# Opening stage of a fused backbone layer: where x is loaded, when the modulation weights are asked for, and where the first modulation chain stands

## The chip, the core and the metric

One NeuronCore of a Trainium2 chip runs the kernel. Its engines are TensorE (PE; its weight loads are PEld in the profile), VectorE (DVE), ScalarE (ACT), GpSimd (POOL) and SyncE (SP); SP, POOL and ACT also hand transfers to the core's 16 DMA engines. Each engine works through its own list of instructions in order and waits on semaphores. The metric is the device time of one launch in microseconds, lower is better.

## What is computed

One layer of a diffusion backbone on 256 latent and 256 context tokens of width 2048. The part that matters here is its start:

```python
mod = jax.nn.silu(c) @ w_mod[l] + b_mod[l]
shift, scale, gate = jnp.split(mod[:, None, :], 3, axis=-1)
mod_c = jax.nn.silu(c_ctx) @ w_mod[l] + b_mod[l]
...
h = _layer_norm(x) * (1.0 + scale) + shift
h_c = _layer_norm(ctx) * (1.0 + scale_c) + shift_c
aq, ak, av, az, bq, bk, bv, bz, bg, mga, mgb = _split_cols(h @ w_in[l])
```

Behind it come neighbourhood attention, a gated linear attention in two directions, branch gates, a merge, the output projection and a layer norm. The change touches none of that.

## The kernel before

Tokens and channels are cut in 128s; a channel tile is a k-tile (kt 0 to 15, `KT`). Every projection splits its operands into a rounded part and the rest (hi and lo) and makes three matmuls: hi by hi, hi by the weights' lo, lo by hi. `mm` (line 137) issues a matmul, `split` (L140) makes hi on ACT and lo on DVE, `load` (L146) asks SP for a weight tile (`raw`, four buffers) and splits it.

The opening runs so:

- SP asks for the four 128-row tiles of x and context (`row`, 1 MB each), then for the modulation weights of k-tile 0 in two halves (`wm0_0`, `wm0_1`, 1 MB each; `load_mod`, L186). `xt`, `row` and `wm` tiles share one pool of eight 8 KB buffers (`k8`), so later `wm` halves and some `xt` tiles wait until a `row` tile has been read.
- PE transposes x (L225) into PSUM, ACT copies it out to `xt` (L226); DVE takes the statistics of the rows (L229, L230). Reciprocal deviation and mean (`rsn`) are spread over columns, transposed on PE (`st`, L247) and copied to `stat`: the first half by DVE (L251), the second by ACT (L249).
- `normalise(kt)` (L253) makes two 512-wide passes on DVE over a part of `xt` (L255, L256).
- `modulate(kt)` (L264) makes the modulation vectors of a k-tile: 16 matmuls `gp` against the two `wm` halves (L138 by way of `mm`; the trace shows each as two), a DVE copy `gs` (L273), two transposes on PE (L275), three small DVE steps `md` (L278, L281, L282), two ACT passes `h` (L285) and a `split` into `hhi` and `hlo`.
- The key projection (L300 to L313): per k-tile seven outputs (`kp`, `K0` = 7) of three matmuls each, with weights `ak` (448 KB per k-tile, tiles `r_ak`, `h_ak`, `l_ak`). In front of k-tile kt's matmuls stands the preparation of kt+1, and the `wm` halves of kt+2 are asked for by POOL, once the `gp` matmuls that read the old contents of a buffer are done.

The order on each engine is not written by hand. A scheduler of the tile framework places the instructions from the order of the code, priorities and `tc.issue_after`, which keeps an instruction behind another one. In the text below gp0, kp0, ak1 and so on carry the number of their k-tile (kp: of the output).

```python
    for kt in range(KT):
        if kt + 1 < KT:
            pend.append(load(wak[kt + 1], P * K0, f"ak_{kt + 1}", begun))
            normalise(kt + 1)
            ...
            modulate(kt + 1)
        wh, wl = pend[kt]
```

Of the kernel before, what the change touches and what calls it, by code (L numbers as in the profile page):

```python
# [16 lines left out]
P = 128  # L17
# [69 lines left out]
def tile_backbone_layer(  # L87
# [84 lines left out]
    hlo = hpool.tile([P, 2, KT, T], F32R, tag="hlo", name="hlo")  # L172
    xh, xl = hhi[:, 0], hlo[:, 0]
# [9 lines left out]
    rows = [k8([P, D], f"row{i}") for i in range(4)]  # L183
# [6 lines left out]
    for i in range(4):  # L190
        nc.sync.dma_start(rows[i][:], xin[i])
# [25 lines left out]

    mvs = tiny([P, 4, 2], "mvs", 1)
    for i in range(4):
        cols = slice(P * i, P * i + P)  # L220
        for c in range(4):
            tp = acc(f"xt{i}_{c}")
            for k in range(4):
                kt = 4 * c + k
                nc.tensor.transpose(tp[:, P * k : P * k + P], rows[i][:, P * kt : P * kt + P], ident[:])  # L225
            evac = nc.scalar.copy(xts[c][:, :, cols], tp[:].rearrange("p (k t) -> p k t", k=4))  # L226
        st = tiny([P, 4, 6], "st")
        for c in range(4):
            nc.vector.bn_stats(st[:, c, :], rows[i][:, 512 * c : 512 * c + 512])  # L229
# [32 lines left out]
    turned = []  # L262

    def modulate(kt):  # L264
        gp = bank(f"gp{kt}")
        for q in range(2):
            wm = wms[kt, q]
            for i in range(8):
                g = 32 * (i % 4)
                with tc.issue_after(turned[-1]) if turned else nullcontext():  # L270
                    mm(gp[g : g + 32, :T], scp[:, 8 * q + i, :], wm[:, i, :], q == 0 and i < 4, q == 1 and i >= 4)
        gs = k2([P, T], f"gs{kt}")
        nc.vector.tensor_copy(gs[:], gp[:, :T])  # L273
# [599 lines left out]
```

## Time and profile before

| | |
|---|---|
| median of 3 runs | 1288.79 us (1288.2 to 1289.65) |
| profiled execution, span | 1287.8 us |
| median less that span | 1.0 us |
| PE busy | 1251.3 us (97%) |
| DVE busy | 744.9 us (58%) |
| ACT busy | 521.6 us (40%) |
| POOL busy | 87.3 us (7%) |
| read from HBM | 222.49 MB, 174 GB/s over the span |

How to read it: the span runs from the first to the last instruction of one profiled execution, and the durations below come from that one. Matmuls are pipelined, so a busy PE can still hold short gaps, and the duration of one matmul is longer than the distance to the next. The first of the page's 40 slices is the only one in which PE is less than nine tenths busy (6 tenths).

### The profile page before, as it was taken

The page shows a single profiled execution, that of the slowest core. Times are in us where ns is not written, and L with a number is a line of the kernel's source. Part 1 is how long each engine was busy: PE and PEld are TensorE (multiplying, and loading weights), DVE is VectorE, ACT ScalarE, POOL GpSimd, SP SyncE. Part 2 cuts the span into 40 slices and gives each one's busy share as a digit, 9 for nine tenths or more (in the row PEclk, how much of TensorE's full clock was granted, in tenths as well). Part 3 has the DMA queues.
Part 4 walks back from the last instruction along what each step waited for, and adds up shares of the span by engine and source line. Part 5 has one row for each costly group of instructions (what it writes and reads, how often), then busy time and mean ns, then how long its engine had stood idle before and what let it go on. Part 6 is the DMA issues. An engine that isn't in the chain of part 4 may idle for free.

```text
span 1287.8 us, 20740 instructions
## 1 busy us (share of the span) xinstructions
PE 1251.3 (97%) x8548; PEld 1124.1 (87%) x8548; DVE 744.9 (58%) x1111; ACT 521.6 (40%) x752; POOL 87.3 (7%) x120
## 2 busy tenths in 40 slices
PE   6999999999999999999999999999999999999994
PEld 4767999976678898888888999999999999999784
DVE  6733322676659456465484668865455454555576
ACT  5333322444454333332442644443444434445341
POOL 1111000111110010010020000000000000000123
PEclk8999999999999999999999999999999999999997
DMA  9997333555435325334244378875666655667652
GB/s 380 400 397 286 90 96 105 165 131 134 129 98 164 98 86 177 97 102 145 82 132 133 119 223 265 282 239 181 182 182 185 187 182 181 182 184 255 236 180 76
DMA packets 61440, 230.15 MB, mean 179 GB/s; under 512 B 7376, under 2 KB 7904, under 8 KB 56224
## 3 DMA queue, kind: packets, MB, share of 16 engines
q1 hardware_dynamic: 53424, 189.83, 47.0%
q0 software_dynamic: 7488, 38.68, 8.1%
q8 instruction: 67, 1.10, 0.4%
q10 hardware_dynamic: 432, 0.30, 0.1%
q14 instruction: 29, 0.24, 0.1%
HBM read 222.49 MB, written 2.10 MB: 174 GB/s over the span
## 4 chain that ended last, share of the span: by engine, by line
PE 88%; DVE 5%; DMA 4%; issue 2%; ACT 1%; POOL 0%; DVEq 0%; SPq 0%; ACTq 0%; POOLq 0%
PE bv L138 14%; PE mga L138 7%; PE mgb L138 7%; PE va L138 7%; PE pb L138 7%; PE kp L138 7%; PE bk L138 6%; PE bz L138 6%; PE wo L138 4%; PE qp L138 4%; PE pa L138 4%; PE az L138 3%; PE gp L138 2%; PE o L138 2%; PE s L138 2%
## 5 line engine op out<-in xcount | busy, mean ns | idle before, releaser
L138 PE MATMUL bv<-l_bv,hhi 128*128 128x512 f32 x256 | 100.0, 391 | 1.0 <-DVE l_bv L144 1.0
L138 PE MATMUL bv<-h_bv,hhi 128*128 128x512 f32 x256 | 99.7, 389 | 0.0
L138 PE MATMUL bv<-h_bv,hlo 128*128 128x512 f32 x256 | 99.6, 389 | 0.0
L138 PE MATMUL bz<-hhi,l_bz 128*128 128x256 f32 x256 | 72.6, 283 | 0.7 <-DVE l_bz L144 0.7
L138 PE MATMUL mga<-hhi,h_mga 128*128 128x256 f32 x256 | 72.4, 283 | 0.0
L138 PE MATMUL mga<-hhi,l_mga 128*128 128x256 f32 x256 | 72.4, 283 | 0.0
L138 PE MATMUL mga<-hlo,h_mga 128*128 128x256 f32 x256 | 72.4, 283 | 0.0
L138 PE MATMUL mgb<-hhi,h_mgb 128*128 128x256 f32 x256 | 72.4, 283 | 0.0
L138 PE MATMUL mgb<-hhi,l_mgb 128*128 128x256 f32 x256 | 72.4, 283 | 0.0
L138 PE MATMUL mgb<-hlo,h_mgb 128*128 128x256 f32 x256 | 72.4, 283 | 0.0
L138 PE MATMUL pb<-hhi,h_pb 128*128 128x256 f32 x256 | 72.4, 283 | 0.0
L138 PE MATMUL pb<-hhi,l_pb 128*128 128x256 f32 x256 | 72.4, 283 | 0.0
L138 PE MATMUL pb<-hlo,h_pb 128*128 128x256 f32 x256 | 72.4, 283 | 0.0
L138 PE MATMUL bz<-hhi,h_bz 128*128 128x256 f32 x256 | 72.4, 283 | 0.0
L138 PE MATMUL bz<-hlo,h_bz 128*128 128x256 f32 x256 | 72.4, 283 | 0.0
L144 DVE TENSOR_TENSOR l_pb<-r_pb,h_pb 128x1024 fp32r<-128x1024 f32 x32 | 39.2, 1225 | 51.1 <-ACT h_pb L142 51.1
L138 PE MATMUL va<-h_av,hlo 128*128 128x352 f32 x192 | 62.1, 323 | 0.0
L138 PE MATMUL va<-h_av,hhi 128*128 128x352 f32 x192 | 61.9, 322 | 0.0
L138 PE MATMUL va<-l_av,hhi 128*128 128x352 f32 x192 | 61.7, 322 | 0.0
L144 DVE TENSOR_TENSOR l_mga<-r_mga,h_mga 128x1024 fp32r<-128x1024 f32 x32 | 39.2, 1225 | 35.6 <-ACT h_mga L142 35.6
L481 DVE SCALAR_TENSOR_TENSOR gacc<-wg,sc,gacc 128x1024 f32<-128x1024 f32 x32 | 41.1, 1284 | 32.2 <-DMA wg<-in_wgate 32.2
L138 PEld LDWEIGHTS bv<-l_bv,hhi 128*128 128x128 f32 x256 | 48.1, 188 | 11.6 <-DVE l_bv L144 1.9
(308 smaller groups left out, 3878.9 us busy)
## 6 DMA issues: line engine op xcount, KB each, us to landing
wm<-in_wmod POOLq DMA_DIRECT2D x28, 1024.0 KB, 9.3
r_bv<-in_wst SPq DMA_DIRECT2D x32, 512.0 KB, 3.6
wg<-in_wgate SPq DMA_DIRECT2D x32, 512.0 KB, 4.3
r_bz<-in_wst SPq DMA_DIRECT2D x32, 512.0 KB, 4.5
r_mga<-in_wst SPq DMA_DIRECT2D x32, 512.0 KB, 3.5
r_mgb<-in_wst SPq DMA_DIRECT2D x32, 512.0 KB, 3.6
r_pb<-in_wst SPq DMA_DIRECT2D x32, 512.0 KB, 3.6
r_wo<-in_wst SPq DMA_DIRECT2D x28, 512.0 KB, 4.2
```

The lines of the kernel that those rows point to most:

```text
L138: nc.tensor.matmul(o, a, b, start=start, stop=stop)
L144: nc.vector.tensor_tensor(out=lo, in0=src, in1=hi.bitcast(F32), op=ALU.subtract)
L481: nc.vector.scalar_tensor_tensor(half, raw[:], sc[:, n // 2, 0:1], half, ALU.mult, ALU.add)
```

## The change

Four edits to the opening, nothing behind it:

- the four x tiles become one tile `rows` in the memory in which `hlo` is made later (`hlo` is now allocated after the statistics), so they no longer take `k8` buffers;
- the `wm` halves of k-tile 1 are asked for on SP behind `ak_0`; `ak_1` and those behind it come after them;
- `modulate` is cut into `modulate` (matmuls of one half), `vectors` (copy, transposes, `md`) and `modulated` (`h` and its split). gp0's matmuls stand ahead of the `st` transposes; the two `st` tiles become one pair tile; k-tile 0's vectors get a higher priority;
- the preparation of k-tile 1 (`prepare(1)`) stands inside k-tile 0's key matmuls, behind the first two outputs; the weights `ak` are split only behind the preceding k-tile's `hhi` and `hlo`.

```diff
-    hlo = hpool.tile([P, 2, KT, T], F32R, tag="hlo", name="hlo")
-    xh, xl = hhi[:, 0], hlo[:, 0]
+    rows = hpool.tile([P, 4, D], F32, tag="hlo", name="rows")
...
-    rows = [k8([P, D], f"row{i}") for i in range(4)]
...
-        nc.sync.dma_start(rows[i][:], xin[i])
+        nc.sync.dma_start(rows[:, i, :], xin[i])
...
+    turned = []
+
+    def behind(ins):
+        return tc.issue_after(ins) if ins is not None else nullcontext()
+
+    def modulate(kt, q, gp):
+        if q == 0:
+            gp = bank(f"gp{kt}")
+        wm = wms[kt, q]
+        for i in range(8):
+            g = 32 * (i % 4)
+            with behind(turned[-1] if turned else None):
+                mm(gp[g : g + 32, :T], scp[:, 8 * q + i, :], wm[:, i, :], q == 0 and i < 4, q == 1 and i >= 4)
+        return gp
+
+    def vectors(kt, gp, after=None):
+        gs = k2([P, T], f"gs{kt}")
+        with behind(after):
+            nc.vector.tensor_copy(gs[:], gp[:, :T])
+        for c in range(2):
+            t = nc.tensor.transpose(gp[:, T + P * c : T + P * c + P], gs[:, P * c : P * c + P], ident[:])
+        turned.append(t.ins)
+        md = tiny([P, 2, 2], "md")
...
+        return md
+
+    def modulated(kt, md):
+        h32 = k2([P, 2, T], f"h32_{kt}")
...
+        return split(hhi[:, :, kt, :], hlo[:, :, kt, :], h32[:])
...
+    hlo = hpool.tile([P, 2, KT, T], F32R, tag="hlo", name="hlo")
+    xh, xl = hhi[:, 0], hlo[:, 0]
+    gp0 = modulate(0, 0, None)
     stat = k4([P, 2, 512], "stat")
+    sps = pair("st")
     for j in range(2):
-        sp = bank(f"st{j}")
+        sp = sps[:, j, :]
...
     begun = (stat_act, stat_dve)
+    normalise(0)
+    modulate(0, 1, gp0)
+    with tc.high_priority(offset=60):
+        md = vectors(0, gp0, stat_dve)
+        made = [modulated(0, md)]
     pend = [load(wak[0], P * K0, "ak_0", begun)]
     for q in range(2):
         load_mod(1, q, nc.sync)
-    normalise(0)
-    modulate(0)
+
+    def prepare(kt):
+        after = made[-1]
+        pend.append(load(wak[kt], P * K0, f"ak_{kt}", after))
+        if kt + 1 < KT:
+            for q in range(2):
+                dma = load_mod(kt + 1, q, nc.gpsimd)
+        normalise(kt)
+        gp = modulate(kt, 0, None)
+        modulate(kt, 1, gp)
+        made.append(modulated(kt, vectors(kt, gp, after[1])))
+        return dma if kt + 1 < KT else None
+
     for kt in range(KT):
-        if kt + 1 < KT:
...
-            modulate(kt + 1)
+        if 0 < kt < KT - 1:
+            mod_dma = prepare(kt + 1) or mod_dma
         wh, wl = pend[kt]
         for p in range(K0):
+            if kt == 0 and p == 2:
+                turned.append(ins)
+                mod_dma = prepare(1)
```

The order that the scheduler makes of it, at three places. First SP's list of transfers, from the x rows on; `r_ak_1` is the raw weight tile of k-tile 1, `wm1_0` the first half of its modulation weights. Before:

```order
L188 DMA wm0_1_107<-in_wmod 128x2048
L148 DMA r_ak_0_278<-in_wak 128x896 [waits DMAHW0_49]
L148 DMA r_ak_1_320<-in_wak 128x896 [waits DMAHW1_49]
L148 DMA r_ak_2_383<-in_wak 128x896 [waits DMAHW2_49]
L188 DMA wm1_0_284<-in_wmod 128x2048 [waits DMAHW3_49,DMAHW4_49,DVE_49,PE_49]
L188 DMA wm1_1_286<-in_wmod 128x2048 [waits DMAHW5_49,DVE_49,PE_49]
L148 DMA r_ak_3_446<-in_wak 128x896
```

and with the change:

```order
L187 DMA wm0_1_103<-in_wmod 128x2048
L149 DMA r_ak_0_306<-in_wak 128x896 [waits DMAHW0_49]
L187 DMA wm1_0_312<-in_wmod 128x2048 [waits DMAHW1_49]
L187 DMA wm1_1_314<-in_wmod 128x2048 [waits DMAHW2_49]
L149 DMA r_ak_1_322<-in_wak 128x896 [waits DMAHW3_49]
L149 DMA r_ak_2_379<-in_wak 128x896 [waits DMAHW4_49]
L149 DMA r_ak_3_442<-in_wak 128x896 [waits DMAHW5_49]
```

The waits of `wm1` on DVE and PE are gone, and both halves stand ahead of `r_ak_1` and `r_ak_2`. POOL's list is the same in both: `wm2_0` behind gp0's first half, `wm2_1` behind its second.

Second, PE from the last x transposes to gp2 (`gp1_332<-wm1_0_284` is the first half of gp1). Before, gp0 stood behind all `st` transposes, gp1 and its transposes ahead of the first kp, and gp2 behind 21 kp. With the change the first part reads

```order
L266 MATMUL xt3_3_223<-ident_73,rows_90 128x128 x3
L138 MATMUL gp0_246<-wm0_0_101,scp_111 32x256 [waits DMAHW6_49,DVE_49]
L138 MATMUL gp0_246<-wm0_0_101,scp_111 32x256 x7
L138 MATMUL gp0_246<-wm0_1_103,scp_111 32x256 [waits DMAHW7_49]
L138 MATMUL gp0_246<-wm0_1_103,scp_111 32x256 x7
L292 MATMUL st_256<-ident_73,col0_257 128x128 [waits DVE_49] x4
L292 MATMUL st_256<-ident_73,col1_267 128x128 [waits DVE_49,Activation_49]
L292 MATMUL st_256<-ident_73,col1_267 128x128 [waits Activation_49] x3
L237 MATMUL gp0_246<-ident_73,gs0_293 128x128 [waits DVE_49]
```

and, behind seven kp,

```order
L138 MATMUL gp1_334<-wm1_0_312,scp_111 32x256 [waits DMAHW1_49]
L138 MATMUL gp1_334<-wm1_0_312,scp_111 32x256 x7
L138 MATMUL gp1_334<-wm1_1_314,scp_111 32x256 [waits DMAHW2_49]
L138 MATMUL gp1_334<-wm1_1_314,scp_111 32x256 x7
L138 MATMUL kp2_279<-hhi_89,l_ak_0_309 128x512
L138 MATMUL kp2_279<-hlo_245,h_ak_0_308 128x512
L138 MATMUL kp3_280<-hhi_89,h_ak_0_308 128x512 [waits PE_49]
L237 MATMUL gp1_334<-ident_73,gs1_351 128x128 [waits DVE_49]
```

with eleven kp more before gp2. The `st` transposes of the second half (`col1`) now wait for DVE as well: for its copy of the first half out of the pair tile.

Third, DVE around the copy of gp1. Before:

```order
L144 TENSOR_TENSOR l_ak_2_386<-r_ak_2_383,h_ak_2_385 128x896 [waits DMAHW2_49,Activation_49]
L282 TENSOR_SCALAR md_311<-md_311 128x2 [waits DVE_49]
L255 TENSOR_TENSOR xt0_93<-xt0_93,stat_249 128x512
L273 COPY gs1_349<-gp1_332 128x256 [waits PE_49]
L256 TENSOR_TENSOR xt0_93<-xt0_93,stat_249 128x512 [waits DVE_49]
```

with the change:

```order
L144 TENSOR_TENSOR hlo_245<-h32_0_301,hhi_89 128x2x256 [waits Activation_49]
L144 TENSOR_TENSOR l_ak_1_325<-r_ak_1_322,h_ak_1_324 128x896 [waits DMAHW3_49,Activation_49]
L301 TENSOR_TENSOR xt0_93<-xt0_93,stat_255 128x512 [waits DVE_49]
L300 TENSOR_TENSOR xt0_93<-xt0_93,stat_255 128x512
L300 TENSOR_TENSOR xt1_94<-xt1_94,stat_255 128x512
L235 COPY gs1_351<-gp1_334 128x256 [waits PE_49]
```

`l_ak_1`, which needs the landing of `r_ak_1` (DMAHW3) and ACT's cast `h_ak_1`, and three passes stand ahead of gs1's copy; before, the three `l_ak` ahead of it were those whose weights SP had asked for in front of `wm1`.

## Rows read from the trace of the kernel before

**Rows 1.** The page's first part: busy time, share of the span and number of instructions of TensorE and its weight loads, then the other engines.

```profile
PE 1251.3 (97%) x8548; PEld 1124.1 (87%) x8548; DVE 744.9 (58%) x1111; ACT 521.6 (40%) x752; POOL 87.3 (7%) x120
```

**Rows 2.** The chain of waits of the first 140 us in order of time: start us, length us, what.

```profile
16.82 11.62 DMA wm<-in_wmod
...
31.66 6.23 PE kp L138 x21
37.88 1.86 PE gp L138 x32
39.75 1.12 PE kp L138 x4
40.87 0.22 PE gp L275 x2
41.09 3.89 PE kp L138 x17
...
130.12 1.86 PE gp L138 x32
```

**Rows 3.** Busy time in four stretches of the opening: stretch (us from the span's start), its length, busy us and instructions of PE, PEld, DVE, ACT and POOL, granted TensorE clock as a share of full speed, busy share of the DMA engines, GB/s.

```profile
16.05:18.95 2.90, 0.00 (x0) 0.00 (x0) 2.19 (x11) 1.85 (x6) 0.00 (x0) 1.00 0.99 409
...
20.95:24.35 3.40, 3.37 (x32) 1.63 (x24) 2.64 (x4) 2.59 (x4) 0.72 (x1) 0.50 1.06 433
...
27.75:31.20 3.45, 2.17 (x17) 0.83 (x18) 1.18 (x3) 1.68 (x3) 0.46 (x1) 0.50 1.00 407
31.20:34.60 3.40, 3.40 (x10) 2.73 (x10) 3.22 (x9) 0.74 (x2) 0.07 (x1) 0.51 1.05 430
```

**Rows 4.** Waits of PE from 13 to 40 us: who waited for whom, us in total, times, longest us.

```profile
PE gp L138 <- DMA wm<-in_wmod: 2.2, 1, 2.2
```

**Rows 5.** The same columns as rows 3 for three longer stretches; the last column is the rate of the transfers in GB/s.

```profile
0.00:25.00 25.00, 14.90 (x105) 11.85 (x106) 16.95 (x41) 17.37 (x31) 2.88 (x12) 0.93 0.92 372
0.00:30.00 30.00, 17.70 (x138) 12.90 (x138) 20.16 (x47) 19.08 (x34) 3.58 (x13) 0.91 0.94 379
5.00:25.00 20.00, 14.90 (x105) 11.85 (x106) 16.76 (x40) 13.66 (x27) 1.08 (x2) 0.91 1.02 421
```

**Rows 6.** Instructions of DVE, then of ACT, in order of time: start us, length us, engine, line, operation, and in brackets the idle time before it and what ended that. An instruction's length reaches a little into the next one's.

```profile
16.78 0.26 DVE L230 BATCH_NORM_AGGREGATE mvs<-st 128x2 f32<-128x24 f32 x1
...
19.96 0.69 DVE L251 COPY stat<-st 128x512 f32<-128x512 f32 x1 [0.47 <-PE st L247]
...
25.70 0.17 DVE L278 TENSOR_REDUCE md<-gp 128x4 f32<-128x16 f32 x1
...
26.46 1.08 DVE L144 TENSOR_TENSOR l_ak<-r_ak,h_ak 128x896 fp32r<-128x896 f32 x1
27.46 0.16 DVE L282 TENSOR_SCALAR md<-md 128x2 f32<-128x2 f32 x1
...
30.48 0.42 DVE L273 COPY gs<-gp 128x256 f32<-128x256 f32 x1 [2.27 <-PE gp L138]
...
31.78 0.68 DVE L255 TENSOR_TENSOR xt<-xt,stat 128x512 f32<-128x512 f32 x1
32.38 0.68 DVE L144 TENSOR_TENSOR hlo<-h,hhi 128x512 fp32r<-128x512 f32 x1
...
20.44 0.58 ACT L249 COPY stat<-st 128x512 f32<-128x512 f32 x1 [0.42 <-PE st L247]
...
27.72 1.09 ACT L285 ACTIVATE h<-xt,md 128x256 f32<-128x256 f32 x2 [4.17 <-DVE md L282]
28.84 0.62 ACT L142 CAST hhi<-h 128x512 fp32r<-128x512 f32 x1
...
37.92 0.94 ACT L142 CAST h_ak<-r_ak 128x896 fp32r<-128x896 f32 x1 [2.32 <-PE kp L138]
```

**Rows 7.** Transfers of modulation weights. In pairs: the issue (start us, length us, queue, line), and under it the answer on that issue, whose last number is the time from issue to landing in us. First wm0's halves on SP, then wm2's on POOL.

```profile
3.37 0.45 SPq L188 DMA_DIRECT2D wm<-in_wmod  x1
wm<-in_wmod SPq DMA_DIRECT2D x1, 1024.0 KB, 12.8
...
3.85 0.49 SPq L188 DMA_DIRECT2D wm<-in_wmod  x1
wm<-in_wmod SPq DMA_DIRECT2D x1, 1024.0 KB, 14.8
...
22.93 0.72 POOL L188 DMA_DIRECT2D wm<-in_wmod  x1 [20.50 <-PE gp L138]
wm<-in_wmod POOLq DMA_DIRECT2D x1, 1024.0 KB, 9.3
...
24.64 0.53 POOL L188 DMA_DIRECT2D wm<-in_wmod  x1 [0.99 <-DMA wm<-in_wmod]
wm<-in_wmod POOLq DMA_DIRECT2D x1, 1024.0 KB, 11.2
```

**Rows 8.** Instructions of PE in order of time, columns as in rows 6. A `gp` matmul counts twice.

```profile
12.73 3.32 PE L225 MATMUL xt<-ident,row 128*128 128x128 f32 x26
...
24.84 0.44 PE L275 MATMUL gp<-ident,gs 128*128 128x128 f32 x2 [0.52 <-DVE gs L273]
25.21 1.07 PE L138 MATMUL gp<-wm,scp 128*32 128x256 f32 x16
...
31.31 0.78 PE L138 MATMUL kp<-hhi,h_ak 128*128 128x512 f32 x1
```

More of the change, by code (lines that the diff above doesn't have):

```diff
@@ L137, in mm @@
     def mm(o, a, b, start, stop):
-        nc.tensor.matmul(o, a, b, start=start, stop=stop)
+        return nc.tensor.matmul(o, a, b, start=start, stop=stop).ins
     def split(hi, lo, src, after=None):
         with tc.issue_after(after[0]) if after else nullcontext():
-            nc.scalar.copy(hi, src)
+            cast = nc.scalar.copy(hi, src)
         with tc.issue_after(after[1]) if after else nullcontext():
-            nc.vector.tensor_tensor(out=lo, in0=src, in1=hi.bitcast(F32), op=ALU.subtract)
+            sub = nc.vector.tensor_tensor(out=lo, in0=src, in1=hi.bitcast(F32), op=ALU.subtract)
+        return cast.ins, sub.ins
     def load(src, n, name, after=None):
@@ L216, in rstd_of @@
         return r
+    turned = []
[18 more added lines that the diff above has]
+        md = tiny([P, 2, 2], "md")
+        nc.vector.tensor_reduce(
+            md[:], gp[:, T:].rearrange("p (c g m) -> p c m g", c=2, g=4)[:, :, 0:2, :], AX.X, ALU.add
+        )
+        nc.vector.tensor_tensor(out=md[:], in0=md[:], in1=bm[:, kt], op=ALU.add)
+        nc.vector.tensor_scalar(md[:, 0, :], md[:, 0, :], 1.0, None, ALU.add)
+        return md
+    def modulated(kt, md):
+        h32 = k2([P, 2, T], f"h32_{kt}")
+        for s in range(2):
+            nc.scalar.activation(
+                h32[:, s, :],
+                xts[kt // 4][:, kt % 4, T * s : T * s + T],
+                AF.Identity,
+                scale=md[:, 0, s : s + 1],
+                bias=md[:, 1, s : s + 1],
+            )
+        return split(hhi[:, :, kt, :], hlo[:, :, kt, :], h32[:])
     mvs = tiny([P, 4, 2], "mvs", 1)
@@ L228, in tile_backbone_layer @@
         for c in range(4):
-            nc.vector.bn_stats(st[:, c, :], rows[i][:, 512 * c : 512 * c + 512])
+            nc.vector.bn_stats(st[:, c, :], rows[:, i, 512 * c : 512 * c + 512])
         nc.vector.bn_aggr(mvs[:, i, :], st[:])
@@ L248, in tile_backbone_layer @@
         if j:
-            stat_act = nc.scalar.copy(stat[:, j, :], sp[:]).ins
+            stat_act = nc.scalar.copy(stat[:, j, :], sp).ins
         else:
-            stat_dve = nc.vector.tensor_copy(stat[:, j, :], sp[:]).ins
+            stat_dve = nc.vector.tensor_copy(stat[:, j, :], sp).ins
     def normalise(kt):
@@ L312, in tile_backbone_layer @@
             mm(kdst[p], wl[:, c], hhi[:, 0:2, kt, :], False, False)
-            mm(kdst[p], wh[:, c], hlo[:, 0:2, kt, :], False, kt == KT - 1)
+            ins = mm(kdst[p], wh[:, c], hlo[:, 0:2, kt, :], False, kt == KT - 1)
     def project_t(name, dst, n, ah, al, kt=KT):
```

37 lines of the change are left out of this document (1 added, 36 removed).

## The prediction

> **What bounds the kernel now.** The engine table comes first: PE is busy 1251.3 us, 97% of the span [rows 1], so a change pays only by what it does to the moment from which PE runs without a gap. The chain of waits shows that moment. Its early pieces are a DMA, the second half of wm1, asked for at 16.82 us and 11.62 us on its way, then gp1 on PE, then 21 kp matmuls from 31.66, then gp2 at 37.88 [rows 2]. From there PE repeats itself: 1.86 for gp, 1.12 and 3.89 for 21 kp, 0.22 for two transposes, 7.09 us per k-tile, until gp15 at 130.12 with nothing but PE in between [rows 2]. So the start of gp2 is the point to watch: whatever the opening does, the end moves by what gp2's start moves, as long as everything that gp3 and its followers need still comes in time. Next I read stretches of the opening: PE does nothing from 16.05 to 18.95, and its granted clock is 0.50 (1.2 of 2.4 GHz) from 20.95 to 24.35 and again from 27.75 to 34.60 [rows 3]. Ahead of gp1's second half it waits 2.2 us for wm, the wait that the chain names [rows 4]. All the while the DMA engines are full: 421 GB/s from 5 to 25 us [rows 5].
>
> **Part 1, memory.** The x rows now lie where hlo will lie, so the eight 8 KB buffers hold four xt and four wm. SP may ask for wm1 in the first microseconds and no longer waits until the statistics and transposes have let go of the x rows. hlo's first write comes long after the rows were read, and costs nothing. ACT's third and fourth evacuation no longer wait for a row buffer; that is worth nothing either, since DVE's statistics are ready only at 17.04 (16.78 + 0.26) [rows 6], and the two small ACT steps behind them are as before.
>
> **Part 2, the first chain.** gp0 now stands ahead of the st transposes on PE. Its first half has to wait for wm0_0 (3.37 + 12.8 = 16.2 us) and its second for wm0_1 (3.85 + 14.8 = 18.65) [rows 7]; 16 of its pieces took 1.07 us at full clock [rows 8], so it ends at 19.7. That fills the idle stretch at 16 to 19. Then four st0 transposes (26 took 3.32, so 0.51 [rows 8]) end at 20.2, the DVE copy of stat takes 0.69 [rows 6], to 20.9; this is 0.3 later than now. A wait is added here: st1 lies in the same pair tile and its four transposes come only after that copy, 0.5 us at full clock and about 1.0 at half, to 21.5 or 22.0; ACT's copy adds 0.58 [rows 6]. gs0's copy (0.42) follows on DVE at once, its transposes (0.44 [rows 8]) stand behind st1 and end at 21.9 or 22.7. From the reduce to the end of md DVE took 1.92 us (25.70 to 27.46 + 0.16) with one 512-wide pass and one l_ak between; now two passes stand there. A pass holds DVE 0.60 (31.78 to 32.38), an l_ak 1.00 (26.46 to 27.46) [rows 6], so 1.5: md is ready at 23.5 or 24.2. Two h activations (1.09) and the cast (0.62) [rows 6] give hhi at 25.3 or 26.0. The first kp starts then, at 25.4 or 26.1, not at 31.31 [rows 8]: 5.2 to 5.9 us sooner.
>
> **Part 3, what that head start still has to pay.** Before, gp1 was over when kp began. Now 7 kp, gp1, 3 kp, gs1's transposes and 11 kp come before gp2: 5.01 + 1.86 + 0.22 = 7.09 us at full clock [rows 2]. Alone this puts gp2 at 32.5 to 33.2; with the clock at half from 26.1 until some 31.2 (a half stretch of the same sort as in [rows 3]) the loss is 2.55 and gp2 stands at 35.75, 2.1 ahead of 37.88.
>
> **Part 4, the step that I think decides.** On DVE, gs1's copy stands behind l_ak_1 and three passes, and l_ak_1 needs ak1, which SP now asks for behind both halves of wm1. On PE, gs1's transposes stand in the middle of k-tile 0. When does ak1 land? Ahead of it, and with it, SP's queue carries 4 MB of rows, wm0 2, ak0 0.44, wm1 2 and ak1 0.44 (in units of 1024 KB): 9.31e6 bytes. POOL asks for wm2's halves as soon as gp0's halves are done, at 17.4 and 19.8, not at 22.93 and 24.64. These took 9.3 and 11.2 us to land [rows 7], so they would land at 26.7 and 31.0, and nearly all of wm2, 2.10e6 bytes, passes before ak1 is in. That makes 11.41e6; the first 30 us moved 379 GB/s x 30 = 11.37e6 [rows 5]. ak1 therefore lands at about 30.4 (estimate: 30.1 and 0.3 to land). Without any of wm2 ahead it would be 25.3 (372 x 25 = 9.30e6 [rows 5]). Between these ends I take 30.4, since POOL's own landings lie around it. The row on the rate is 421 GB/s. The Trainium skill, page "DMA: Bandwidth & Descriptors", section Specifications, has an HBM limit per core of about 358 GB/s; by it ak1 would be 4 us later still, and the sum 4 us worse. The trace disagrees, with 421, and the measurement decides.
>
> From 30.4: the cast of h_ak_1 0.94 [rows 6], to 31.4; l_ak_1 1.0, to 32.4; three passes 1.8, to 34.2; gs1 0.42, to 34.6. PE has gp1 and the three kp behind it done by 32.7 even at half clock, and sits idle for 2 us or more. From 34.6 it does 0.22 and 11 kp at 5.01 / 21 = 0.239, together 2.85, and gp2 starts at 37.5. So 5 us of head start shrink to 0.4.
>
> **Part 5, the clock.** Both idle stretches of the opening, 2.9 and 2.2 us long, were followed by half clock, for 3.4 and for 6.85 us [rows 3, 4]. The new wait is as long, and behind it PE has no gap, so a stretch at half costs half its length. Bounds: 0 and 3.4 us; I take the shorter stretch, 1.7, since PE works through the whole of it. gp2 at 39.2, 1.3 later than 37.88.
>
> **The sum.** A head start of 5.2 to 5.9 us; less gp1 and its transposes, 2.1; less the clock before 31.2 and the wait for gs1, 2.7 to 3.4 more than the clock now costs between 31.31 and 37.88, which leaves 0.4 at gp2; less 1.7 of clock: +1.3 us. Later work covers the rest. hhi_1 is ready some 3.9 us after gs1, at 38.5, and gp2 ends at 41.0; wm3, asked for at 31 to 32, needs 11 us as the rows above and is wanted at 46; the order behind the opening is the same instruction by instruction. Against the profiled execution (span 1287.8) this gives 1289.1; the median of the runs is 1.0 above that span, so **1290.1 us**.
>
> **The rivals.** *The clock holds* (0.22): no fall after the wait, gp2 at 37.5, -0.4 us, 1288.4. The clock rows speak against it, by two of two. The Trainium skill, page "TensorE: Matmul & The Clock Gate", section HAM oscillation, speaks for it: it tells of a kernel that loses its clock to waits for DMA longer than this one, and by that rule this wait would be free. The trace disagrees, with a fall after 2.2 us, though one execution is little.
> *The change does what its title says* (0.13): ak1 lands near 25.3, DVE is not held, and only PE's list counts. With the half clock of part 3, gp2 at 35.75, -2.1 us, 1286.7 (0.08). With the full clock throughout, gs1 is ready at 30.2 and gp2 starts at 30.3 + 2.85 = 33.1, -4.8 us, 1284.0 (0.05). For it speaks only that POOL's first transfer may start late; its 9.3 us to land are more than its bytes need.
> *Slower, beyond the noise* (0.10): the clock falls during the wait and stays at half for 6.85 us, as it did from 27.75 to 34.60. From 34.6 the 2.85 take 5.7, gp2 starts at 40.3 and runs half of its time slow too, 3.4 lost in all: -0.4 + 3.4 = +3.0 us, 1291.8. It decides when the half stretch lasts past 40 us.
> *The forecast* (0.55): 1290.1.
>
> **How the numbers follow.** 0.2% of 1288.8 is 2.6 us, about what a measurement of this kernel can tell from no change: faster means under 1286.2, slower over 1291.4. Faster: 0.05 for the full clock and a part of the 0.08 around -2.1, with something for a landing between the ends: 0.11. Slower: 0.10 and the tail of the forecast, 0.12. Same: 0.77. The range reaches from the undelayed case at half clock to the long fall, 1286.6 to 1291.9; the forecast alone has 1289.3 to 1291.0.
>
> **What would show it.** In the profile after: first kp between 25 and 26.5; PE waiting about 2 us for gs1's copy near 33 to 35, and DVE waiting some 4 us for h_ak_1 with the landing of ak1 behind it; ak1 in at 30 to 31; clock 0.5 for a stretch that begins near 34; gp2 at 39 against 37.88; then 7.09 per k-tile as before. The prediction is wrong if ak1 lands before 28, if PE shows no wait at gs1, or if a k-tile after gp2 takes other than 7.09.

## The result: 0.4 per cent slower, and the profile after

The changed kernel takes 1292.38 us (median of 5 runs, 1291.15 to 1294.65); the kernel before, beside it on the same chip, 1288.71 (5 runs, 1286.91 to 1289.65). The ratio is 1.0037, 95% interval 1.0022 to 1.0052: slower, and 0.5 us beyond the upper end of the range. The profiled execution took 1293.62, with a span of 1291.9, which is 4.1 more than that of before. The medians lie 3.7 apart, where +1.3 was forecast. The page's engine line, against [rows 1]:

```profile
PE 1250.9 (97%) x8548; PEld 1125.2 (87%) x8548; DVE 745.4 (58%) x1111; ACT 521.3 (40%) x752; POOL 87.3 (7%) x120
```

PE is busy for the same time (1250.9 against 1251.3 us); what grew is the time in which it does nothing. (Of the 40 slices the last is short too, 4 tenths in both kernels, which the section on the time before left out; it is the kernel's end, and the change doesn't reach it.) The chain of waits of the changed kernel says where (start us, length us, what; against [rows 2]). Its starts are some 0.07 us later than those of the same instructions in the lists of instructions further down:

```profile
9.19 23.51 DMA r_ak<-in_wak
32.72 0.95 ACT h_ak L142
33.69 1.09 DVE l_ak L144
34.78 0.60 DVE xt L301
35.39 1.20 DVE xt L300 x2
36.59 0.34 DVE gs L235
36.98 0.69 PE gp L237 x2
37.67 4.69 PE kp L138 x11
42.36 2.03 PE gp L138 x32
...
134.83 1.86 PE gp L138 x32
```

Read it from the top: the transfer of ak1 (r_ak is its raw tile), ACT's cast of it, l_ak_1, three passes, gs1's copy, gs1's transposes, 11 kp, gp2. It is the forecast's chain, name by name. But gp2 starts at 42.36, not at 39.2, and at 37.88 before; gp15 is 4.7 us later than before (134.83 against 130.12), and the span 4.1.

The waits of PE in the first 50 us (who waited for whom, us in total, times, longest), and below them DVE's longest from 20 to 50:

```profile
PE gp L237 <- DVE gs L235: 5.0, 1, 5.0
PE kp L138 <- ACT hhi L142: 3.5, 1, 3.5
PE gp L138 <- DMA wm<-in_wmod: 1.6, 2, 1.3
PE st L292 <- DVE stat L296: 0.9, 1, 0.9
...
DVE l_ak L144 <- ACT h_ak L142: 6.8, 1, 6.8
```

The 2.2 us wait for wm1 ahead of gp1 [rows 4] is gone. In its place PE stands 5.0 us at gs1's transposes, because DVE stood 6.8 us at l_ak_1. The head start is real: three instructions of PE in order of time, the first kp, gp1 and the last kp ahead of the wait:

```profile
25.99 0.80 PE L138 MATMUL kp<-hhi,h_ak 128*128 128x512 f32 x1 [3.46 <-ACT hhi L142]
...
29.19 1.93 PE L138 MATMUL gp<-wm,scp 128*32 128x256 f32 x32
...
31.62 0.40 PE L138 MATMUL kp<-hhi,h_ak 128*128 128x512 f32 x1
```

The first kp at 25.99 stands against 31.31 [rows 8]. Stretches of the opening (columns as in [rows 3]; granted clock third from the end):

```profile
24.00:27.80 3.80, 1.81 (x4) 1.49 (x5) 2.90 (x6) 1.71 (x3) 0.00 (x0) 0.71 1.00 406
27.80:31.20 3.40, 3.40 (x37) 1.74 (x36) 0.00 (x0) 0.00 (x0) 0.53 (x1) 0.82 1.00 408
31.20:34.60 3.40, 0.82 (x3) 0.34 (x3) 0.91 (x1) 0.94 (x1) 0.53 (x1) 1.00 1.04 417
34.60:38.00 3.40, 1.02 (x4) 0.93 (x5) 3.22 (x8) 0.00 (x0) 0.00 (x0) 0.69 1.01 415
38.00:41.40 3.40, 3.40 (x10) 2.63 (x9) 3.40 (x8) 2.10 (x4) 0.00 (x0) 0.50 0.56 228
41.40:44.00 2.60, 2.60 (x31) 1.16 (x33) 1.84 (x3) 0.45 (x1) 0.13 (x1) 0.75 0.00 1
```

From 31.2 to 38 PE is busy for 1.84 of 6.8 us; then the clock is at 0.50 (1.2 GHz) while it works. Two transposes and 11 kp take 5.4 us (36.98 to 42.36) where they need 2.85 at full clock. The last row shows the other side: the transfers have nothing left to do (1 GB/s).

### The profile page after: what moved, and what is told of

It reads as the page before. It is cut to its first block, busy times and chain, and to the rows that moved or that the text cites. A ratio compares the mean times of both kernels' runs of the same rounds, so it can differ in the third digit from the quotient of the medians.

```text
span 1291.9 us, 20735 instructions
## 1 busy us (share of the span) xinstructions
PE 1250.9 (97%) x8548; PEld 1125.2 (87%) x8548; DVE 745.4 (58%) x1111; ACT 521.3 (40%) x752; POOL 87.3 (7%) x120
## 4 chain that ended last, share of the span: by engine, by line
PE 89%; DMA 4%; DVE 4%; issue 2%; ACT 1%; POOL 0%; SPq 0%; DVEq 0%; ACTq 0%; POOLq 0%
PE bv L138 14%; PE mgb L138 7%; PE mga L138 7%; PE va L138 7%; PE pb L138 7%; PE bk L138 7%; PE kp L138 7%; PE bz L138 6%; PE wo L138 6%; PE pa L138 4%; PE qp L138 3%; PE az L138 3%; PE gp L138 2%; DMA r_ak<-in_wak 2%; PE o L138 2%
## 5 line engine op out<-in xcount | busy, mean ns | idle before, releaser
L144 DVE TENSOR_TENSOR l_pb<-r_pb,h_pb 128x1024 fp32r<-128x1024 f32 x32 | 39.2, 1225 | 51.1 <-ACT h_pb L142 51.1
L144 DVE TENSOR_TENSOR l_mga<-r_mga,h_mga 128x1024 fp32r<-128x1024 f32 x32 | 39.2, 1225 | 34.7 <-ACT h_mga L142 34.7
```

The lines of the kernel that those rows point to most:

```text
L144: sub = nc.vector.tensor_tensor(out=lo, in0=src, in1=hi.bitcast(F32), op=ALU.subtract)
```

## The experiments

The theory after the result: *ak1's landing holds l_ak_1, l_ak_1 holds gs1's copy on DVE, gs1 holds PE, and PE's clock falls in the wait.* The rivals: the clock alone makes gp2 late; the transfers are late as a whole, whatever the order; the pair tile of st is the new wait. One variant after another takes away one link. Each ratio is to the kernel before, run beside that variant's group on the same chip (medians 1286.4 to 1286.9 us), with a 95% interval; each profile is of one execution.

**The changed kernel once more.**

> The changed kernel once more, unaltered, to stand beside the other kernels of this group on the same chip, and to show whether the landing of ak1 and the fall of the clock repeat. Theory: ak1 lands at 31.5 to 33 us, PE waits 4 to 5.2 us for gs1's copy, the clock is at half from about 36 on for 5 us or more, gp2 starts at 41 to 43; ratio to the kernel before 1.002 to 1.005. Rival (that execution was an accident of one landing): ak1 near 30.4 as forecast, gp2 near 39, ratio 0.999 to 1.002.

Measured: ratio 1.0050 (1.0031 to 1.0069). The cast of h_ak_1 starts at 32.58, PE's wait is 4.4 us, gp2 starts at 41.33:

```profile
36.84 0.58 PE L237 MATMUL gp<-ident,gs 128*128 128x128 f32 x2 [4.37 <-DVE gs L235]
...
41.33 1.93 PE L138 MATMUL gp<-wm,scp 128*32 128x256 f32 x32
```

So the landing repeats to 0.14 us. The clock repeats only roughly: transposes and 11 kp took 4.5 us here, 1.6 over full clock, against 2.5 over it in the first profile.

**The kernel before once more.**

> The kernel before, unaltered, profiled once more. The three variants of the changed kernel that start gp2 at 35.3 to 35.8 came out level with the kernel before or 0.1 per cent faster, where 2.1 to 2.5 us at gp2 would give 0.2 per cent. Theory (the opening of the kernel before is the same in every execution, and what differs between runs lies behind gp15): gp2 at 37.5 to 38.2 with half clock ahead of it, gp15 near 130, as in the first profile. Rival (the clock in the opening of the kernel before is a matter of luck): gp2 at 35 to 36.5, with the clock at 1.00 from 28 to 34 us, where the first profile had 0.50.

Measured (one profiled run, 1286.47, span 1284.8): the rival is right on the clock and on gp2's first half, and misses the wait inside gp2. The rows are its stretches after 24 us and PE's two halves of gp2:

```profile
24.00:27.80 3.80, 2.10 (x34) 0.82 (x30) 3.60 (x9) 0.20 (x2) 1.42 (x3) 1.00 1.01 412
27.80:31.20 3.40, 2.83 (x25) 1.63 (x18) 3.04 (x8) 1.71 (x3) 0.53 (x1) 1.00 1.00 400
31.20:34.60 3.40, 3.40 (x16) 2.58 (x15) 3.40 (x7) 1.72 (x3) 0.00 (x0) 1.00 1.02 420
```

```profile
34.65 1.07 PE L138 MATMUL gp<-wm,scp 128*32 128x256 f32 x16
37.37 1.07 PE L138 MATMUL gp<-wm,scp 128*32 128x256 f32 x16 [1.65 <-DMA wm<-in_wmod]
```

The clock that was 0.50 from 27.75 to 34.6 in [rows 3] was 1.00 here, after a wait of PE for wm1 of 1.15 us instead of 2.2. gp2 began 3.2 us sooner and then stood for wm2: with the clock up, the transfers bound this opening, and gp15 came 1.4 us sooner, at 128.69. Of the two falls that the prediction counted, the first came again (0.50 from some 20.2 to 23.6, after an idle stretch of 3.3 us); the second, the one ahead of gp2, is not in every execution of the kernel before.

**ak1 asked for ahead of wm1.**

```diff
+    early = {1: fetch(wak[1], P * K0, "ak_1")}
     for q in range(2):
         load_mod(1, q, nc.sync)
...
-        pend.append(load(wak[kt], P * K0, f"ak_{kt}", after))
+        pend.append(load(wak[kt], P * K0, f"ak_{kt}", after, early.get(kt)))
```

> The changed kernel, with one thing else: SP asks for ak1 ahead of the two halves of wm1 and no longer behind them. Theory (the landing of ak1 holds h_ak_1 and l_ak_1, l_ak_1 holds gs1's copy on DVE, gs1 holds PE, and PE's clock falls in that wait): ak1 lands at 20 to 22 us and not at 32.7, since 7.2e6 bytes and not 11.4e6 stand ahead of its last; DVE's idle 6.8 us ahead of l_ak_1 and PE's 5.0 us ahead of gs1's transposes are gone; wm1 lands about 1.1 us later, so PE waits that much longer ahead of gp1; gs1's copy near 32.2, gp2 at 34.8 with the clock up and 37.5 with it down, against 42.4 in the changed kernel and 37.9 in the kernel before. Time 5 to 7.5 us below the changed kernel's, which is 0.3 to 3 below the kernel before: ratio to the kernel before 0.9975 to 0.9998. Rival A (the clock alone: the late start comes from waits of PE wherever they are, and gp1's longer wait does as well): gp2 at 39 or later, ratio 1.001 or more. Rival B (the transfers are late as a whole and order only moves the lateness): gp1 ends 2 us or more later than 31.1 and gp2 comes at 39 to 41, ratio 1.001 to 1.002.

Measured: ratio 0.9998 (0.9988 to 1.0007). l_ak_1 and gs1's copy on DVE:

```profile
26.61 1.09 DVE L144 TENSOR_TENSOR l_ak<-r_ak,h_ak 128x896 fp32r<-128x896 f32 x1
...
32.26 0.42 DVE L239 COPY gs<-gp 128x256 f32<-128x256 f32 x1 [2.76 <-PE gp L138]
```

DVE now waits for PE at gs1, not PE for DVE, and gp2 starts at 35.76. gp1 got no later wm1: it ran slowly (3.1 us) because the clock was at 0.50 until some 31.5, from the other idle stretch ahead of the first kp. Rivals A and B are out.

**gs1's copy ahead of l_ak_1, every transfer as in the changed kernel.**

```diff
+        raw = fetch(wak[kt], P * K0, f"ak_{kt}")
+        if kt > 1:
+            pend.append(load(None, P * K0, f"ak_{kt}", after, raw))
...
+        md = vectors(kt, gp, after[1])
+        if kt == 1:
+            pend.append(load(None, P * K0, f"ak_{kt}", (after[0], last_md[0]), raw))
+        made.append(modulated(kt, md))
```

> The changed kernel, every transfer asked for in its order, but h_ak_1's cast and l_ak_1 are put behind k-tile 1's last md step on DVE, so that gs1's copy stands ahead of them. Theory: ak1 lands as late as in the changed kernel, 32 to 33 us; gs1's copy comes at 31.1, right behind gp1; PE's 5.0 us wait ahead of gs1's transposes falls to 0.5 or less; gp2 at 34.2 (full clock) to 36.5 (half clock from some point), and a smaller wait shows instead ahead of k-tile 1's kp, for l_ak_1 or hhi_1, at 36 to 38. Time 4 to 8 us below the changed kernel's, ratio to the kernel before 0.997 to 1.000. Rival A (the transfers: what holds PE is data that come late, not an order on DVE): the wait moves in full to k-tile 1's kp, 4 us or more there, and the time stays within 1.5 us of the changed kernel's, ratio 1.002 to 1.004. Rival B (the clock alone): gp2 at 39 or later, half clock from 36 on as in the changed kernel.

Measured: ratio 0.9987 (0.9976 to 0.9998). DVE in this variant:

```profile
31.88 0.42 DVE L240 COPY gs<-gp 128x256 f32<-128x256 f32 x1 [2.12 <-PE gp L138]
...
34.61 1.09 DVE L144 TENSOR_TENSOR l_ak<-r_ak,h_ak 128x896 fp32r<-128x896 f32 x1
```

This is the edit that settles it. ak1 lands as late as ever (its cast starts at 32.50), but gs1's copy no longer stands behind it: PE has no wait at gs1, none at k-tile 1, and gp2 starts at 35.37, 7 us sooner than in the changed kernel. ak1 was never late for its own matmuls; it was late for a place on DVE that had been given to it too early.

**wm2 asked for by SP, behind ak1.**

```diff
-                dma = load_mod(kt + 1, q, nc.gpsimd)
+                dma = load_mod(kt + 1, q, nc.sync if kt == 1 else nc.gpsimd)
```

> The changed kernel, with the two halves of wm2 asked for by SP, behind ak1, and no longer by POOL. Theory, with the part of it that says why ak1 is late (POOL's wm2 takes the DMA engines from ak1 although ak1 was asked for 9 us earlier): ak1 lands at 25 to 27 and not at 32.7; l_ak_1 is done by 28 and gs1's copy follows gp1 at 31.2; gp2 at 34.5 to 37; wm2 lands at 30 to 33 and k-tile 1 has no new wait for it. Time 4.5 to 7 us below the changed kernel's, ratio to the kernel before 0.9975 to 1.0. Rival (POOL's queue has no part in it; ak1 is late because of what stands ahead of it on SP's own queue): ak1 lands at 31 or later still, DVE and PE wait as in the changed kernel, ratio 1.002 to 1.005.

Measured: ratio 0.9996 (0.9985 to 1.0008). DVE:

```profile
28.59 1.09 DVE L144 TENSOR_TENSOR l_ak<-r_ak,h_ak 128x896 fp32r<-128x896 f32 x1 [1.83 <-ACT h_ak L142]
...
31.81 0.42 DVE L235 COPY gs<-gp 128x256 f32<-128x256 f32 x1 [0.32 <-PE gp L138]
```

The cast starts at 27.62 instead of 32.72: POOL's wm2, asked for 9 us after ak1, had cost it 5.1 us. gp2 at 35.30, as the theory wanted; the landing missed its upper bound by 0.6. That remainder had to be looked at (the last experiment).

**PE kept busy in the wait for gs1.**

```diff
+        for i in range(22 if kt == 1 else 0):
+            mm(kdst[6], pend[0][0][:, :P], hhi[:, 0:2, 0, :], True, True)
         for c in range(2):
             t = nc.tensor.transpose(gp...
```

> The changed kernel, with 22 further 128x512 matmuls on PE between gp1 and gs1's transposes, into kp6's bank, whose first real matmul overwrites them; the three kp matmuls that stood between gp1 and the transposes come behind them. The 22 take about 5 us at full clock, which is the length of PE's wait for gs1. Theory (the fall of the clock is a price of its own beside the wait, and comes from PE doing nothing): ak1 and gs1's copy are as late as in the changed kernel (32.7 and 36.5), but the granted clock stays over 0.9 from 33 to 41 where it was 0.50 to 0.75, so two transposes and 14 kp take 3.6 us and gp2 starts at 40.2 to 41 against 42.4: time 1.3 to 2.3 us below the changed kernel's. Rival A (the clock falls at this place whatever PE does): gp2 at 43 or later, since three kp more stand behind the transposes at half clock; time 0 to 1.5 us above the changed kernel's. Rival B (the fall costs nothing because something else is late at gp2): gp2 starts as in the changed kernel and waits for wm2.

Measured: ratio 1.0061 (1.0046 to 1.0075). At gp2 the theory holds, in the time it fails. PE of this variant:

```profile
31.35 5.33 PE L138 MATMUL kp<-hhi,h_ak 128*128 128x512 f32 x22
36.52 0.38 PE L239 MATMUL gp<-ident,gs 128*128 128x128 f32 x2
...
40.86 1.93 PE L138 MATMUL gp<-wm,scp 128*32 128x256 f32 x32 [0.74 <-DVE md L242]
43.99 0.50 PE L138 MATMUL kp<-hhi,h_ak 128*128 128x512 f32 x1 [1.19 <-ACT hhi L142]
```

The clock was 1.00 in all three stretches from 31.2 to 41.4, and two transposes and 14 kp took 3.6 us (36.52 to 40.12), where two and 11 had taken 5.4 and 4.5, so that gp2 began at 40.86 even after a wait of 0.74. (ak1's cast and gs1's copy came 1.1 us sooner here than in the changed kernel, 31.70 and 35.49; PE was still in the 22 matmuls, so gp2 gained nothing by it.) But the added matmuls changed the order on DVE behind gs1: the reduce of k-tile 1 came behind eight passes, at 40.64, and k-tile 1's kp waited for hhi_1; gp3 started at 52.41 where the changed kernel has 49.58. Between gp2 and gp3 lie waits of PE of 2.3 us in all, and behind them the clock was at 0.50 again, from some 47.1 to 50.5, for 1.7 us more. The price of the clock is shown at gp2; the variant is slower by another place on DVE, and by the fall that came with it.

**The x rows alone, in the kernel before.**

```diff
+    rows = hpool.tile([P, 4, D], F32, tag="hlo", name="rows")
-    rows = [k8([P, D], f"row{i}") for i in range(4)]
...
-        nc.sync.dma_start(rows[i][:], xin[i])
+        nc.sync.dma_start(rows[:, i, :], xin[i])
```

> The kernel before with one part of the change alone: the x rows lie in the memory of h's low parts. The order of the modulations and the order on POOL stay as they were. SP then asks for wm1 in the first microseconds, and for ak1 and ak2 behind it, where the kernel before had both ak ahead of wm1's wait; on DVE l_ak_1 and l_ak_2 stand ahead of the last md steps of k-tile 0. Theory (an ak that lands late holds DVE, and with it PE): ak1 lands at 27 to 32, l_ak_1 holds md of k-tile 0 behind it, the first kp comes at 33 to 36 (31.3 in the kernel before), gp2 at 39 to 43, time 1 to 6 us above the kernel before, ratio 1.001 to 1.005. Rival (wm1's early request is the gain, the hold is peculiar to the changed order of the modulations): first kp at 28 to 30, gp2 at 35 to 36, ratio 0.997 to 0.999.

Measured: ratio 1.0012 (1.0002 to 1.0021), the sign of the theory, its places missed: ak1's cast started at 26.05, the first kp at 31.23, gp2 at 37.81. The waits of DVE from 20 to 40 us and of PE from 0 to 50:

```profile
DVE l_ak L144 <- ACT h_ak L142: 2.6, 2, 1.8
```

```profile
PE gp L275 <- DVE gs L273: 3.0, 2, 2.4
```

Asking for wm1 early took away the wait for it, and l_ak_1 and l_ak_2 on DVE put 2.4 us at gs1 in its place. Behind that wait the clock was at 0.50 once more, from some 32.4 to 35.9. Freed memory alone gains nothing with DVE in this order, which had been made for ak ahead of wm1.

**Banks of their own for the st tiles, on the variant with gs1's copy first.**

```diff
-    sps = pair("st")
...
-        sp = sps[:, j, :]
+        sp = acc(f"st{j}")[:]
```

> The variant that puts gs1's copy ahead of l_ak_1, with the two st tiles in banks of their own (those that the kp take later) and not in one pair tile, so that st1's transposes need not wait for the copy of st0. Theory (the pair tile's wait of 0.9 us is real, but stands ahead of gs0 on a stretch that only sets the first kp): the 0.9 us wait of st for stat is gone; the first kp starts 0.3 to 0.9 us sooner, at 25.0 to 25.6 against 25.85; gp2 0.3 to 0.9 us sooner than the 35.4 of that variant; the time 0 to 0.9 us lower, inside the interval. Rival (the wait is what makes the head start small): gp2 1.5 us or more sooner.

Measured: ratio 0.9994 (0.9982 to 1.0006). The waits of PE from 0 to 50 us:

```profile
PE kp L138 <- ACT hhi L142: 4.0, 1, 4.0
...
PE gp L242 <- DVE gs L240: 0.9, 1, 0.9
```

A miss: st's 0.9 us wait is gone, and PE waits the same 0.9 at gs0 instead; with l_ak_0 put ahead of the last md step, the first kp came at 26.20, later by 0.36. The pair tile costs at most some 0.1 us here (md's reduce at 22.29 with banks of their own, 22.42 without), since gs0's copy is what PE needs next in either case.

**PE kept busy ahead of the first kp, on the variant with wm2 on SP.**

```diff
         made = [modulated(0, md)]
+        for i in range(24):
+            c = P * (i % 4)
+            with behind(turned[-1]):
+                nc.tensor.transpose(kdst[6][:, c : c + P], xts[3][:, 3, c : c + P], ident[:])
```

> The variant in which SP asks for wm2 behind ak1, and with 24 further 128x128 transposes on PE between gs0's transposes and the first kp, into kp6's bank, which is overwritten later. There PE was idle for 3.45 us (22.4 to 25.85), the clock fell to 0.50 at 23.85 and was back only at 30.7, although PE worked through from 25.85. Theory (the clock falls because PE does nothing, and its price is half of the stretch at half in which PE works): the 24 take 3.1 us by the rate of the xt transposes and end before hhi_0 is there; the granted clock stays over 0.9 from 20 to 34; the first kp starts at 25.9 as it did; gp1 ends at 29.5 to 30 and not 31.7; gp2 at 32.9 to 33.6 and not 35.3, unless it waits for wm2, which landed near 33; 1.7 to 2.4 us below that variant's time, ratio to the kernel before 0.9955 to 0.998. Rival A (the clock is granted by a count of its own, whatever PE does): half clock as before, gp2 at 35.3 or later. Rival B (PE was not the bound there, wm1 and wm2 were): full clock, but PE waits for wm and gp2 stays at 35.

Measured: 1284.36 against 1286.39, ratio 0.9981 (0.9971 to 0.9991); the changed kernel itself, on the same chip, 1293.26. PE:

```profile
21.86 2.78 PE L316 MATMUL kp<-ident,xt 128*128 128x128 f32 x24
25.47 0.50 PE L138 MATMUL kp<-hhi,h_ak 128*128 128x512 f32 x1 [0.83 <-ACT hhi L142]
27.30 1.93 PE L138 MATMUL gp<-wm,scp 128*32 128x256 f32 x32
31.34 0.44 PE L237 MATMUL gp<-ident,gs 128*128 128x128 f32 x2 [1.22 <-DVE gs L235]
```

Two stretches (columns as in [rows 3]), without the 24 transposes and with them:

```profile
24.00:27.80 3.80, 1.95 (x5) 1.56 (x6) 2.76 (x4) 1.89 (x4) 0.00 (x0) 0.50 1.01 415
27.80:31.20 3.40, 3.40 (x32) 1.68 (x34) 2.61 (x4) 0.76 (x1) 0.00 (x0) 0.60 1.00 413
...
24.00:27.80 3.80, 2.96 (x25) 1.97 (x27) 2.38 (x4) 2.11 (x4) 0.00 (x0) 1.00 1.03 421
27.80:31.20 3.40, 2.33 (x31) 1.09 (x23) 3.15 (x5) 0.22 (x1) 1.25 (x2) 1.00 1.00 409
```

With them the granted clock is 1.00 from 16 to 51 us; without them it was 0.50 from some 23.7 to 30.5. (The 23.85 and 30.7 expected above are those of the variant with gs1's copy first.) gp1 ends at 29.2 and not at 31.7. The clock falls because PE does nothing: rival A is out. gp2 came only to 34.24, because with PE that far ahead gs1's copy stood behind l_ak_1 and three passes once more.

**Those two with gs1's copy first.** The edits of the three variants above, together.

> Three edits to the changed kernel together: SP asks for wm2 behind ak1, l_ak_1 stands behind k-tile 1's last md step, and 24 transposes fill PE's idle stretch ahead of the first kp. With the first and the third alone gp1 ended at 29.2 but gs1's copy came at 30.9, behind l_ak_1 and three passes on DVE, and PE waited 1.2 us for it; gp2 at 34.2. Theory (that wait is the order on DVE once more): gs1's copy at 29.2 to 29.9, no wait of PE for it over 0.3 us, clock 1.00 from 20 to 44, gp2 at 32.6 to 33.2, no wait for hhi_1 or l_ak_1 at k-tile 1 over 0.5 us; 1.0 to 1.5 us below that variant, ratio to the kernel before 0.9962 to 0.9978. Rival (with PE so far ahead the transfers decide: wm2's second half, which landed near 33 in the variant without the fill): gp2 waits for wm2 and its second half ends at 35 or later, as it does in that variant; ratio 0.998.

Measured: 1283.01 against 1286.86, ratio 0.9971 (0.9961 to 0.9982), faster than both kernels. PE's waits from 20 to 50 us, all of them:

```profile
PE st L297 <- DVE stat L301: 0.9, 1, 0.9
PE kp L138 <- ACT hhi L142: 0.8, 1, 0.8
```

gs1's copy at 29.71, gp2 at 33.23, gp15 at 125.45.

**Nothing asked for behind ak1.**

```diff
-        raw = stream.tile([P, 1024], F32, tag="raw", name=f"r_{name}", bufs=4)
+        raw = stream.tile([P, 1024], F32, tag="raw", name=f"r_{name}", bufs=2)
...
+        if kt == 1:
+            early[2] = fetch(wak[2], P * K0, "ak_2")
...
+              with behind(asked[0] if kt == 1 else None):
                 dma = load_mod(kt + 1, q, nc.sync if kt == 1 else nc.gpsimd)
```

> The variant that asks for wm2 on SP, with two buffers for raw weights where there were four, and wm2 asked for behind ak2: so nothing is asked for behind ak1 until l_ak_0 is done, near 25. (Later stages have two such buffers too, so only the opening is read.) In that variant ak1 landed at 27.6, when 10.30e6 bytes had moved, though only 9.31e6 stood ahead of ak1's last; in the changed kernel it was 32.7, 12.42e6 and 11.41e6. Theory L (the transfers asked for behind ak1 pass on some of the 16 DMA engines while ak1's last piece is still behind other work on the slowest; taking them away changes nothing for that engine): ak1 lands at 27 to 27.8 again, and the rate of all engines falls below 350 GB/s in the last 2 us ahead of it. Theory S (the later transfers share the engines with ak1 and delay it): ak1 lands at 25.2 to 25.8, at about 9.3e6 bytes, with the rate at 400 GB/s and more up to the end.

Measured: the cast starts at 27.86, theory L. (The time, 1410.93 us in one run, isn't read: the variant has two raw buffers in every stage and not four.) The last column is the rate in GB/s:

```profile
24.00:25.00 1.00, 0.00 (x0) 0.00 (x0) 1.00 (x3) 0.87 (x2) 0.00 (x0) 0.50 0.99 400
25.00:26.00 1.00, 0.07 (x1) 0.07 (x1) 1.00 (x3) 0.84 (x2) 0.00 (x0) 0.50 0.36 128
26.00:27.00 1.00, 1.00 (x3) 0.81 (x4) 0.84 (x2) 0.00 (x0) 0.00 (x0) 0.50 0.83 179
```

With nothing behind it, most of the DMA engines ran dry at 25, and ak1 still was not in. The trace's single DMA records say what it waited for. A transfer on SP's queue ends with 16 records of 4 bytes, which I read as one for each of the 16 DMA engines (the trace doesn't name the engine); for ak1 (us from the span's start, to about 0.1):

```
kernel                  15th record   16th    cast of h_ak_1   16 KB packet on q8
the changed kernel      30.85         -       32.72            25.50
gs1's copy first        30.79         -       32.50            25.29
wm2 on SP               26.02         27.14   27.62            22.61
nothing behind ak1      25.71         27.13   27.86            25.68
x rows alone            25.44         25.58   26.05            29.20
```

(In the first two the 16th can't be told from the records of ak2.) The last piece is 1.1 and 1.4 us behind the 15th in the third and fourth rows, and in the first two the cast starts 1.9 and 1.7 us behind it. In the last row, where the 16 KB packet came after ak1, it is 0.14; in the run with ak1 asked for first, where it came after ak1 as well (25.60), ak1's last two records are 0.10 apart. That packet is a load of instructions, and in the changed kernel's DMA view from 25 to 27 us it is the one of its kind:

```profile
q8 instruction: 1, 0.02, 3.4%
```

It took 1.07 us in the changed kernel and 1.10 with nothing behind ak1. That it holds one DMA engine and with it the last sixteenth of ak1 fits the times; no run moved the packet alone, so it is inferred, not shown. In the third row it was over at 23.70, ahead of ak1's first piece at 23.94, which this reading doesn't explain in full. The Trainium skill, page "DMA: Bandwidth & Descriptors", section "Why a DMA increments its semaphore by 16 and not by 1", has that only the full 16 mean that all data are there; the trace agrees, since the cast starts behind the 16th in the three rows where that can be told. The Trainium skill, page "Runtime: NRT & Kernel Launch", section "Instruction fetch mechanics", calls the cost of crossing a boundary of 16 KiB mostly hidden. No wait of PE or DVE in the lists above is put down to the packet of 1.07 us, which agrees; of a transfer beside it, which here may have paid, that page says nothing.

**All of them on one scale.** If the opening is all that differs, the start of gp15 must give the time. Taken against the second profile of before (128.69), as a share of 1286.9 us:

```
kernel                      gp15 at   from 128.69   so ratio   measured (95% interval)
gs1 first, wm2 SP, fill     125.45    -3.24         0.9975     0.9971 (0.9961 to 0.9982)
wm2 on SP, fill             126.49    -2.20         0.9983     0.9981 (0.9971 to 0.9991)
wm2 on SP                   127.51    -1.18         0.9991     0.9996 (0.9985 to 1.0008)
gs1's copy first            127.52    -1.17         0.9991     0.9987 (0.9976 to 0.9998)
ak1 first                   128.01    -0.68         0.9995     0.9998 (0.9988 to 1.0007)
own banks                   128.03    -0.66         0.9995     0.9994 (0.9982 to 1.0006)
x rows alone                129.98    +1.29         1.0010     1.0012 (1.0002 to 1.0021)
the changed kernel again    133.59    +4.90         1.0038     1.0050 (1.0031 to 1.0069)
22 matmuls in the wait      137.42    +8.73         1.0068     1.0061 (1.0046 to 1.0075)
```

Every interval holds the value from gp15. But the base was chosen with the results known. With the first profile of before as base (130.05 in its list of instructions), four of the nine values fall outside their interval: wm2 on SP, ak1 first, x rows alone and the changed kernel again. For the second speaks that its execution (1286.47) lies at the median of its kernel (1286.39), while the first's (1289.65) was the slowest of its five. Still it is one execution set against medians, and what followed gp15 took from 1154.7 to 1159.6 us in the profiled ones. With this reserve it would answer why the first three variants gained so little: against the first profile they start gp15 2.0 to 2.5 us sooner, but the kernel before itself does so by 1.4 when its clock holds. How often it holds, no run here shows; the 22 to 29 runs of the kernel before beside each group spread from 1284.3 to 1291.1 us.

## Why the prediction was wrong

The mechanism was right; two terms of the sum were mis-sized, in the first profile both to the same side: the landing of ak1 (part 4) and, less, what the clock costs behind the wait (part 5).

- **Parts 1 and 2 held.** The first kp at 25.99 (25.4 to 26.1 given); the wait that the pair tile adds to st1 is there, 0.9 us; no cost from hlo's memory.
- **Part 4, the step called decisive, failed in the landing of ak1**: 30.4 given, 32.72 measured, 32.58 in the second profile. 2.3 of the 3.2 us by which gp2 is later than forecast (42.36 against 39.2) are this. The bytes were counted well: 15 of the 16 records of ak1 were there at 30.85. But the estimate divided all bytes by the rate of all engines, and the cast waits for the last piece, 1.9 us behind that; when ak1 was in, 12.42e6 bytes had moved, not 11.41e6. The 0.3 us "to land" stand on no row; from the last record to the cast it took 0.5 to 0.7. The lower bound failed alike: 25.3 without wm2 ahead, 27.62 measured when wm2 was behind. So the distance of the two, what POOL's wm2 costs ak1 by passing ahead of it, was right at 5.1 us, though POOL asked at 18.16 and 20.57 and not at 17.4 and 19.8; both ends were 2.3 late. In the run with the x rows alone, with the same 9.31e6 bytes on SP's queue up to ak1 and its last record not behind the others, the cast started at 26.05, late by 0.75 only. So some 1.6 of the 2.3 go with the late last piece, and why that is late (the packet of instructions) stays inferred. From the landing to the end of gs1's copy it took 4.2 us, as given (30.4 to 34.6).
- **PE's wait, "2 us or more", was 5.0 (4.4 in the second profile)**: 2.3 from the landing, the rest because PE came to it sooner. gp1 and the kp behind it were done at 32.0; the 32.7 fits half clock from 26.1 to some 31.2, as in part 3, and the clock was at half only from 25.6 to 29.0.
- **Part 5, the clock, was right in kind and near in size**: 1.7 given; 2.5 in the first profile, 1.6 in the second. The bound of 3.4 held. Its reasons were weaker than they looked: the fall ahead of gp2 that it took from the kernel before did not come back in the second profile of that kernel. The runs with matmuls in the idle stretches show the cause that part 5 assumed. Of the rule named under the rival "The clock holds" (the Trainium skill, page "TensorE: Matmul & The Clock Gate", section HAM oscillation, a kernel that loses its clock to waits for DMA) the runs say little: falls behind waits of 5.0 and 4.4 us, and none behind 1.15 and 1.65 in the second profile of before, agree with it; falls came too behind waits as short as those for which the prediction had read it as free, 2.2 us in the first profile of before, and 2.4 and 0.5 with the x rows alone. The wait that was to be free by it became 5.0 us, so it wasn't put to the test.
- **The last two points of the sum held**: 7.09 us per k-tile from gp3 on (gp15 4.7 us later than before, gp2 4.5), and nothing later was late.
- **The rivals.** "Slower, beyond the noise" had the right verdict and its point of decision (half clock past 40 us: it lasted to some 42.7 in the first profile, to some 40.4 in the second), but it put the loss on the clock alone (3.4 us, with ak1 in at 30.4): that its 1291.8 is the nearest of the numbers is in part luck. "The change does what its title says" is what the variants show once l_ak_1 no longer holds gs1: gp2 at 35.3 to 35.8 with its half clock (35.75 given), and 33.23 with the clock held (33.1 given). "The clock holds" came true in none of the two profiles of the changed kernel. The range ended at 1291.9 because the longest fall and a later landing were never taken together, though the prediction had named a landing 4 us later in a sentence by itself (for a rate of the transfers that the trace contradicts); and "same" had 0.77 with a sum of +1.3 whose two largest terms both had more room upward.

## What to carry to other kernels

A wait on an in-order engine is paid by what is queued behind it: before a transfer is moved back in its queue, look at what stands behind its first reader on every engine, and move that reader too. The landing of a transfer is that of its slowest piece: add a margin to bytes over rate, and where a small transfer decides, ask for it ahead of the large ones. Where PE must wait, matmuls into a bank that is overwritten anyway keep its clock: 24 transposes brought gp15 forward by 1.0 us here, and 22 matmuls put where they changed another engine's order cost more than they gave.

## What the runs showed of the hardware that was not expected

- The same program's opening ran at two clocks: in the kernel before, 0.50 from 27.75 to 34.6 us in one execution and 1.00 in another, with 1.4 us between them at gp15.
- The clock stayed at half long after PE was busy again: from some 23.7 to 30.5 us, with PE at work from 25.85, in the variant with wm2 on SP.
- A later request on POOL's queue took 5.1 us from an earlier one on SP's queue, while the total rate stayed at 400 to 420 GB/s.
